# Eighteen gates slots of seven products instead of fourteen, eleven of them with weight differences made ahead and kept in DRAM

## The chip, the cores and the metric

The kernel runs on one core of one Trainium2 chip. The engines of a core work side by side, each on a queue of its own: TensorE (PE) multiplies matrices from SBUF into the eight PSUM banks, VectorE (DVE) does elementwise work, ScalarE (ACT) does copies and activations, GpSimd (POOL) does next to nothing here, and SyncE (SP) issues nearly all DMAs. The metric is the device time of one execution in microseconds (us), taken as the median of several runs.

## The reference

One decoder block on 256 tokens of width 2048, all in float32:

```python
h = rmsnorm(x, attn_norm_w)
proj = h @ w_in            # 2048 x (4*1024 + 3*1024 + 2*2048)
rq, rk, rv, rg, mq, mk, mv, g_ret, g_moba = split(proj)
o_ret  = silu(rg) * norm(retention(rotary(rq), rotary(rk), rv)) * ret_norm_w   # 4 heads of 256
o_moba = attention(rotary(mq), rotary(mk), mv)                                 # 8 heads of 128, causal
merged = sigmoid(g_ret) * (o_ret @ w_ret_up) + sigmoid(g_moba) * (o_moba @ w_moba_up)
x = x + merged @ w_out
up = causal_dwconv(rmsnorm(x, ffn_norm_w) @ w_ffn_up, conv_w, conv_b)           # 2 * 5632 columns
x = x + (silu(a) * b) @ w_ffn_down                                             # a, b = halves of up
out = rmsnorm(x, final_norm_w)
```

Nearly all of the work is the products with the weights, and each weight is used once.

## The kernel before

**Numbers in two parts.** A float32 operand is split into a high part of PE's faster format and the rest (`split2`: ACT copies the high part, DVE subtracts it and gives the low one). A product is then three matmuls: high by high, low by high, high by low.

**Slots.** The weights come as a stream of *halves*, tiles of 128 x 1024 (512 KB). Two halves are one *slot*, and the whole kernel is 252 slots in an order written out by hand. For a slot `part` splits each half of `raw` into `whi` and `wlo` and issues the load of the half four further on (`load`); there are four buffers of each kind, so the split of slot n+1 runs beside the matmuls of slot n. In a slot come, in the order of issue: the splits for the next slot, sums that are due, one stage of each running task (`run_tasks`), stages of preparation, and then the slot's matmuls, with the small matmuls of the tasks in the middle of them.

**The order of the stages.**

| slots | work |
|---|---|
| 0 to 55 | the heads: 14 groups of 4 slots, in the order mqk0, mv0, mqk2, mqk4, mv1, mqk6, rv0, rg0, rqk0, rqk1, rqk2, rqk3, rv1, rg1 |
| 56 to 103 | four chunks of 12: 8 slots of the two gates (`gr`, `gm`), 4 of the up projections (`um`, `ur`) |
| 104 to 119 | `w_out` |
| 120 to 207 | `w_ffn_up`, 22 groups of 4 slots |
| 208 to 251 | `w_ffn_down` |

A group of heads accumulates in PSUM over its four slots. There are two buffers of two banks each for this (`first_pair`); a q/k group (mqk, rqk) has 512 columns twice and takes both, `acc` and `more`. In a q/k slot the matmuls of `acc` come first and those of `more` second. When a group's last slot is issued, `closed` issues what reads the banks: for a q/k group `summed`, once for `acc` and once for `more` (ACT copies one half of the columns, L421, and DVE adds the other half to it, L422); for mv and rv copies by ACT; for rg the activation Silu by ACT (L694). The attention of the heads then runs as tasks over the next slots. The first norm also is a task: it loads the rows of x (`xt`), squares them on ACT (L376), takes the power on POOL (L289), and spreads the result with the small matmuls `across` in slot 8.

**Slots of seven.** In the gates, in `w_out` and in the down part two products over 256 rows by two column blocks are one 2 x 2 block product, and some slots make it with seven products instead of eight: 21 matmuls of 512 columns instead of 24. Such a slot needs sums of the activations (`seven_sums`, kept in tiles `s`) and, of the slot's four weight blocks, four differences. `seven_parts` makes these *in place*: four subtractions on DVE of 128 x 512 (L756 to L759) in the slot ahead, then the splits of the two halves and of three more blocks (`th`, `tl`). `SEVEN_GATES` names the slots of each chunk, `SEVEN_OUT` those of `w_out`.

**Made ready.** In the down part most slots of seven have their differences from DRAM. `make_ready` fetches a slot's weights into a tile `b`, makes the four differences with three subtractions (L187, L189, L191), and stores them in `differences`; this runs in the slots of `w_ffn_up`, one subtraction a slot. When the slot's turn comes, the three extra blocks are loaded into `got` and split, and the fourth difference is loaded in the place of a quarter of `raw`.

Of the kernel before, what the change touches and what calls it, by code (L numbers as in the profile page):

```python
# [90 lines left out]

SEVEN_GATES, SEVEN_OUT = ((4, 6), (0, 2, 4, 6), (0, 2, 4, 6), (0, 2, 4, 6)), ((3, 5), (2, 4))

# [40 lines left out]
def block(ctx: ExitStack, tc: tile.TileContext, a):  # L134
# [11 lines left out]
    left, right = ExitStack(), ExitStack()  # L146
    dr = ctx.enter_context(tc.tile_pool(name="dr", bufs=1, space=bass.MemoryType.DRAM))
    ctx.enter_context(tc.manual_schedule())

    def pool(stack, name, side="left"):  # L150
        return stack.enter_context(tc.tile_pool(name=name, bufs=1, side=side))

    def f32(ap):
# [16 lines left out]
    down_at = n_halves // 2 - NFB  # L170
    ready = [i for i, (seven, _) in enumerate(down()) if seven and i not in IN_PLACE]
    ready = {2 * (down_at + i): j for j, i in enumerate(ready)}
    differences = dr.tile([len(ready), P, 4 * CW], F32, name="differences")
# [4 lines left out]

    def make_ready(j):

        n = next(n for n, i in ready.items() if i == j)
        b = wq.tile([P, 4, CW], F32, name="b", tag=f"q{j % 2}", bufs=1)
        for h in range(2):
            nc.sync.dma_start(flat(b[:, 2 * h:2 * h + 2, :]), wts[order[n + h]])
        for _ in range(3):
            yield
        nc.vector.tensor_sub(b[:, 1:4:2, :], twice(b[:, 3, :]), b[:, 1:3, :])  # L187
        yield
        nc.vector.tensor_sub(b[:, 2, :], b[:, 2, :], b[:, 1, :])  # L189
        yield  # L190
        nc.vector.tensor_sub(b[:, 0, :], b[:, 0, :], b[:, 2, :])  # L191
        yield
        yield
        nc.sync.dma_start(differences[j], flat(b))

# [4 lines left out]
    def load(n, *some):  # L200
        if n < n_halves:
            if n not in raws:
                raws[n] = rp.tile([P, 2 * CW], F32, name="raw", bufs=RAW_BUFS)
            if n - 1 in ready:
                nc.sync.dma_start(raws[n][:, :CW], wts[order[n], :, :CW])
                nc.sync.dma_start(raws[n][:, CW:], differences[ready[n - 1], :, 3 * CW:])
                return
            for w in some or spans(n):
                nc.sync.dma_start(raws[n][:, w], wts[order[n], :, w])

    def part(n, *some):
# [263 lines left out]
    def retention(fulls, h):  # L475
# [62 lines left out]
        for k, full, w in ks:  # L538
            nc.vector.scalar_tensor_tensor(ot["rl"][:, k, :], full, w, f32(ot["rh"][:, k, :]),
                                           op0=OP.mult, op1=OP.subtract)  # L540

    def flips(full, two, c, gates):

        for b in range(2):
            for i in range(2):
                w = slice((2 * b + i) * P, (2 * b + i + 1) * P)
                for t in range(NT):
                    flip(two[b][:, i * S + t * P:i * S + (t + 1) * P], full[:, t, w])
        yield
        for b in range(2):  # L550
            k = 4 * c + 2 * b
            if gates:
                if len(big["mh"]) == c:
                    big["mh"].append(big["pm"].tile([P, 4, S], F32R, name="mgh3", tag="room", bufs=1))
                split2(*(big["m" + x][c][:, 2 * b:2 * b + 2, :] for x in "hl"), pair(two[b]))
# [110 lines left out]

    def gated():

        return [big["pg"].tile([P, NT, CW], F32, name="s" + x, bufs=1 + (x == "r")) for x in "rm"]

    def middle_pool():
        assert not tasks, len(tasks)
        left.close()
        pm = big["pm"] = pool(left, "pm")
        for x in "hl":
            big["m" + x] = [pm.tile([P, 4, S], F32R, name=f"mg{x}{c}") for c in range(4 - (x == "h"))]
        big["room"] = two_of(pm.tile([P, 2, CW], F32, name="room"))
        big["tt"] = pm.tile([P, 3, CW], F32, name="tt")
        big["junk"] = pm.tile([P, CW], F32, name="junk")
        big["th"], big["tl"] = (pm.tile([P, 3, CW], F32R, name="t" + x) for x in "hl")  # L680

    def closed(kind, n, acc, more):
# [17 lines left out]
        elif kind == "up":  # L700
            if n == 0:
                assert not tasks, len(tasks)
                left.close()
                pf = big["pf"] = pool(left, "pf")
                big["gh"], big["gl"] = (pf.tile([P, NFB - 16, S], F32R, name="g" + x) for x in "hl")
# [44 lines left out]
    def seven_parts(n, tt, th, tl):  # L750
# [10 lines left out]
        split2(*parts[n + 1], q)  # L761
        if isinstance(th, list):
            for one in zip(th, tl, tt):
                split2(*one)
        else:
            split2(th, tl, tt[3])
        for i in range(2):
            load(n + i + RAW_BUFS)

    def three(tile):  # L770
# [154 lines left out]
    def middle_slots(slot):  # L925

        slots = middle()
        fa, fb = two_of(first_pair()), two_of(first_pair())
        sr, sm = gated()
        t124 = [two_of(p1.tile([P, 2, CW], F32R, name="t", tag="kq", bufs=4)) for _ in range(3)]  # L930
        th, tl = [list(x) for x in zip(*t124)]
        for i, (seven, two) in enumerate(slots):
            c, q = divmod(i, 12)
# [17 lines left out]
            if out and q == 3:  # L951
                right.close()
                big["x2"] = [x2_half(wq, f"q{i}") for i in range(2)]
                for k in ("ss2", "ss3"):
# [18 lines left out]
            if i == 8:  # L973
                middle_pool()
                th, tl = big["th"], big["tl"]
                t124 = list(zip(three(th), three(tl)))
            n = 2 * (slot + 1)
            if q == 0 and seven:
                times(r, sr)
            if i + 1 < len(slots) and slots[i + 1][0]:  # L980
                if i < 8:
                    tt = [p1.tile([P, CW], F32, name="tt", tag=x, bufs=2) for x in ("tmp", "tmp", "full")]
                else:
                    tt = three(big["tt"]) + [big["tt"]]
                seven_parts(n, tt, th, tl)
            else:
                part(n)
                part(n + 1)
            if i and q == 0:
                if not seven:  # L990
# [5 lines left out]
                else:  # L996
                    sr, sm = gated()
            if not out:
                if c == 1 and q == 2:
                    seven_sums(3, big["sums"][1][:, 1], "gr")  # L1000
                if c == D // CW - 1 and q >= 10:
                    seven_sums(q - 10, sums_tile(big["pm"], f"s{q - 8}"), "wo")
                if q == 8:
# [7 lines left out]
            else:  # L1011
                if q % 8 == SEVEN_OUT[q // 8][-1] + 1:
                    gather = gathered(at, q // 8 * 2, big["pm"].tile([P, CW], F32, name="v", bufs=1))
                    next(gather)
# [9 lines left out]
            else:  # L1024
                js = (0, 0) if two[0][0] == two[1][0] else (0, 1)
                plain_products([(k, j) for (_, k), j in zip(two, js)], lambda k: two_blocks(k, kind), at, halves)
            issue()
            slot += 1
            if not out and q == 11:
                r, fa, fb, fc = fa, fb, fc, r  # L1030
        for j, bank in ((2, fc), (3, r)):
            summed_up(bank, j)
# [20 lines left out]
    def down_slots(slot):  # L1053
# [4 lines left out]
        th, tl = [big["t"][:, x:x + 3, :] for x in (0, 3)]  # L1058
        t124 = [list(zip(three(th), three(tl)))[x] for x in (1, 2, 0)]
        room = wq.tile([P, 4, CW], F32, name="got", tag="q0", bufs=1)  # L1060
# [3 lines left out]
        for i, (seven, where) in enumerate(slots):  # L1064
# [10 lines left out]
            if next_seven and n not in ready:  # L1075
                assert not seven
                full = big["got"][done % 2]
                seven_parts(n, [three(full)[x] for x in (1, 2, 0)] + [full], th, tl)
                get_differences(done + 2)
# [93 lines left out]
    sevens = [2 * (down_at + i) for i, (seven, _) in enumerate(down()) if seven]  # L1173
    slot, makers = 0, []
    for kind, n, _, _, rows in groups:
        if kind == "gr" and n == 0:
# [11 lines left out]
        for kc in range(nk // 4):  # L1188
            for h in range(2):
                part_x(4 * slot + 4 + 2 * h)  # L1190
                part(2 * slot + 2 + h)
            if kind == "rg" and n == 1 and kc > 0:
                if kc == 1:
# [5 lines left out]
            if kind == "up" and n in SUMS_IN_UP and kc in (1, 3):  # L1199
# [3 lines left out]
                else:  # L1203
                    big["room"] = two_of(big["wb"])
                    seven_sums(k, big["s4"])
            run_tasks()
            if kind == "up":
                j, at = divmod(2 * n + kc - 8, 5)
                if at == 0 and j in ready.values():
                    makers.append(make_ready(j))  # L1210
                for one in list(makers):
                    if next(one, makers) is makers:
                        makers.remove(one)
                if n == NFB - 2 and kc > 1:
                    get_sums(kc - 2, ("wb", "wa")[kc - 2])
            halves = [parts.pop(2 * slot + h) for h in range(2)]
# [80 lines left out]
```

## Time and profile before

| | us |
|---|---|
| median of 3 runs (lowest, highest) | 1412.05 (1412.01, 1412.32) |
| the profiled execution: its time | 1412.28 |
| the profiled execution: its span, first to last instruction | 1410.5 |
| TensorE busy in the span | 1399.3 |
| VectorE busy | 1130.9 |
| ScalarE busy | 782.0 |
| mean granted clock of TensorE | 0.999 |

The page of the profile tells of one execution. Its first part has each engine's busy time, its share of the span and the number of instructions (x). A row of the views by group has the line of the kernel, the engine, the operation, what is written <- what is read, the shapes, and the count; then the busy us, the mean ns of one, and the idle us ahead of them with what ended them. A row of the timeline has the start in us from the span's start, the duration in us, engine, line and operation, and in brackets the idle time ahead and what ended it. A row of the waits has the waiter <- what it waited for, and us in total, times, and the longest. A row of the windows has the stretch, its length, each engine's busy us with its instructions, the granted clock, the DMAs' share, and GB/s. The slots start at the first matmul of each: slot 8 at 51.2, slot 36 at 220.2, slot 40 at 243.7, slot 44 at 268.3, slot 48 at 293.4, slot 56 at 340.8 us.

### The profile page before, as it was taken

The numbers are of one execution on the slowest core, as the hardware profiler recorded it, in microseconds if no ns is written. First come the engines' busy times: TensorE is split into PE (matmuls) and PEld (weight loads), VectorE is DVE, ScalarE is ACT, GpSimd is POOL, SyncE is SP. The second block draws the span as 40 slices with busy tenths as digits, with TensorE's granted clock in tenths as the row PEclk, the third lists the DMA queues.
The fourth block names the chain that finished last, engine by engine and source line by source line (L and its number), as shares of the span: only waits on it lengthen the run. The fifth ranks groups of instructions, "written<-read, shape, count | busy, mean of one in ns | idle before, by whom it ended". The sixth has DMA issues, their size and how long they took to land.

```text
span 1410.5 us, 19509 instructions
## 1 busy us (share of the span) xinstructions
PE 1399.3 (99%) x7194; PEld 1198.2 (85%) x7194; DVE 1130.9 (80%) x1526; ACT 782.0 (55%) x1027; POOL 5.6 (0%) x14
## 2 busy tenths in 40 slices
PE   9999999999999999999999999999999999999997
PEld 7888888888888888888888888888888888888886
DVE  6687656866888989788768898898888988887767
ACT  6555454545556555555556555565555656655653
POOL 0000000000000000000000000000000000000000
PEclk9999999999999999999999999999999999999999
DMA  8755555555566566576486887887787777997894
GB/s 297 265 180 168 172 182 177 171 188 166 193 200 209 190 207 193 194 239 231 161 280 218 289 283 273 292 278 270 260 289 280 257 272 264 344 334 257 292 350 142
DMA packets 92591, 335.22 MB, mean 238 GB/s; under 512 B 10416, under 2 KB 11984, under 8 KB 90448
## 3 DMA queue, kind: packets, MB, share of 16 engines
q1 hardware_dynamic: 92064, 333.19, 69.7%
q8 instruction: 56, 0.92, 0.3%
q10 hardware_dynamic: 432, 0.79, 0.2%
q14 instruction: 39, 0.32, 0.1%
HBM read 308.78 MB, written 25.17 MB: 237 GB/s over the span
## 4 chain that ended last, share of the span: by engine, by line
PE 96%; DMA 1%; DVE 1%; issue 1%; ACT 0%; SPq 0%; POOLq 0%; POOL 0%; DVEq 0%; ACTq 0%
PE acc L235 83%; PE z L235 11%; DMA raw<-in_wts 1%; PE s L235 0%; PE o L235 0%; DVE wlo L227 0%; PE rs L235 0%; PE ro L235 0%; PE z L253 0%; PE acc L253 0%; DVE x L1051 0%; PE pt L253 0%; ACT whi L226 0%; PE tr L253 0%; ACT t L226 0%
## 5 line engine op out<-in xcount | busy, mean ns | idle before, releaser
L226 ACT ACTIVATE whi<-raw 128x1024 fp32r<-128x1024 f32 (+1 forms) x505 | 523.4, 1055 | 411.2 <-PE acc L235 241.8
L227 DVE TENSOR_TENSOR wlo<-raw,whi 128x1024 fp32r<-128x1024 f32 (+1 forms) x505 | 595.5, 1218 | 178.9 <-ACT whi L226 91.5
L235 PE MATMUL acc<-xb,whi 128*128 128x512 f32 x1920 | 466.1, 392 | 1.4 <-ACT whi L226 1.4
L235 PEld LDWEIGHTS acc<-xb,whi 128*128 128x128 f32 x1920 | 350.6, 188 | 68.9 <-ACT whi L226 2.5
L235 PEld LDWEIGHTS acc<-xb,wlo 128*128 128x128 f32 x1920 | 250.9, 191 | 12.2
L235 PE MATMUL acc<-xb,wlo 128*128 128x256 f32 x1920 | 254.6, 282 | 0.0
L235 PE MATMUL acc<-whi,xb 128*128 128x512 f32 x572 | 169.3, 391 | 0.4 <-ACT gate L694 0.4
L235 PEld LDWEIGHTS acc<-whi,xb 128*128 128x128 f32 x572 | 107.3, 188 | 22.8 <-ACT gate L694 0.8
L235 PE MATMUL acc<-wlo,xb 128*128 128x512 f32 x286 | 100.8, 390 | 0.0
L235 PE MATMUL acc<-whi,gl 128*128 128x512 f32 (+1 forms) x202 | 78.2, 387 | 0.0
L235 PE MATMUL acc<-whi,gh 128*128 128x512 f32 (+1 forms) x202 | 78.2, 387 | 0.0
L235 PEld LDWEIGHTS acc<-wlo,xb 128*128 128x128 f32 x286 | 53.8, 188 | 10.6
L235 PE MATMUL acc<-wlo,gh 128*128 128x512 f32 (+1 forms) x202 | 52.5, 387 | 0.0
L227 DVE TENSOR_TENSOR t<-got,t 128x1536 fp32r<-128x1536 f32 x20 | 35.1, 1755 | 15.6 <-PE acc L235 7.9
L235 PEld LDWEIGHTS acc<-wlo,gh 128*128 128x128 f32 x202 | 37.9, 188 | 7.7
L235 PEld LDWEIGHTS acc<-whi,gh 128*128 128x128 f32 x202 | 37.9, 188 | 7.7
L235 PEld LDWEIGHTS acc<-whi,gl 128*128 128x128 f32 x202 | 37.9, 188 | 7.7
L809 ACT ACTIVATE s<-room 128x512 fp32r<-128x512 f32 x16 | 10.1, 634 | 61.2 <-DVE room L806 61.2
L235 PE MATMUL z<-whi,xb 128*128 128x512 f32 x156 | 39.6, 389 | 0.0
L226 ACT ACTIVATE t<-got 128x1536 fp32r<-128x1536 f32 x20 | 29.7, 1486 | 17.3 <-PE acc L235 16.3
L604 DVE SCALAR_TENSOR_TENSOR ub<-ub,vec 128x256 f32<-128x256 f32 x88 | 36.7, 479 | 0.0
L604 DVE SCALAR_TENSOR_TENSOR ua<-ua,vec 128x256 f32<-128x256 f32 x88 | 36.7, 478 | 0.0
(313 smaller groups left out, 1605.4 us busy)
## 6 DMA issues: line engine op xcount, KB each, us to landing
raw<-in_wts SPq DMA_DIRECT2D x488, 512.0 KB, 4.5
b<-in_wts SPq DMA_DIRECT2D x30, 512.0 KB, 7.0
differences<-b SPq DMA_DIRECT2D x15, 1024.0 KB, 8.1
got<-differences SPq DMA_DIRECT2D x15, 768.0 KB, 6.6
s<-sums_kept SPq DMA_DIRECT2D x12, 512.0 KB, 6.9
sums_kept<-s SPq DMA_DIRECT2D x10, 512.0 KB, 6.8
raw<-in_wts SPq DMA_DIRECT2D x17, 256.0 KB, 5.2
raw<-differences SPq DMA_DIRECT2D x15, 256.0 KB, 5.5
```

Of the source, the lines that this page charges most:

```text
L226: nc.scalar.activation(hi, full, AF.Copy)
L227: nc.vector.tensor_sub(lo, full, f32(hi))
L235: to.append(lambda: nc.tensor.matmul(out, a, b, **kw))
L604: nc.vector.scalar_tensor_tensor(y[:, j, :], u[:, j, i:i + S], cv[j][:, i:i + 1], y[:, j, :], op0=OP.mult, op1=OP.add)
L809: nc.scalar.activation(hi, sums, AF.Copy)
```

## The change

Chunk 0 of the gates has slots of seven at 4, 5, 6 (were 4, 6), the other three chunks at 0, 2, 4, 5, 6 (were 0, 2, 4, 6). Of these eighteen, seven are still made in place (`SUMS_AT_ONCE`, counted from the first gates slot: 4, 14, 16, 26, 28, 38, 40), and eleven get their differences from DRAM: slots 5 and 6 of every chunk, and slot 0 of the last three.

The eleven are made in the heads. `PREPARED_AT` has the slot in which each one's three subtractions are issued, now in one piece, behind that slot's tasks and ahead of its matmuls and of `closed`; the fetch (two DMAs of 512 KB) is issued three slots ahead, or two slots behind the subtractions of the last user of the buffer, and the store (1 MB) one slot later. Two new tiles on the right side of SBUF hold first `b` and then `got`. `get_gate` loads three blocks (768 KB) of a ready slot, the first two in slot 55 and each further one when its tile is free; `split_gate` splits them in the slot ahead, ahead of that slot's matmuls or, where that slot is itself one of seven, behind them. The in-place slots use the idle quarter of the `got` tiles and `room` for their temporaries, and split the three blocks one by one.

The sums of the activations for k = 0 and 1 stay in slots 53 and 54; k = 2 goes from slot 55 to the second gates slot, k = 3 from chunk 1 to slot 9 of chunk 0, and k = 4 is new, in slot 10. The sums for `w_out` and some scratch tiles lie elsewhere; the last x tile is taken anew behind the middle (`renew_x`).

```diff
-SEVEN_GATES, SEVEN_OUT = ((4, 6), (0, 2, 4, 6), (0, 2, 4, 6), (0, 2, 4, 6)), ((3, 5), (2, 4))
+SEVEN_GATES, SEVEN_OUT = ((4, 5, 6),) + ((0, 2, 4, 5, 6),) * 3, ((3, 5), (2, 4))
+GATES_AT, SUMS_AT_ONCE = 56, (4, 14, 16, 26, 28, 38, 40)
+PREPARED_AT = (6, 7, 19, 23, 27, 31, 34, 35, 39, 43, 47)
...
+        steps = [
+            fetch,
+            lambda: nc.vector.tensor_sub(b[:, 1:4:2, :], twice(b[:, 3, :]), b[:, 1:3, :]),
+            lambda: nc.vector.tensor_sub(b[:, 2, :], b[:, 2, :], b[:, 1, :]),
+            lambda: nc.vector.tensor_sub(b[:, 0, :], b[:, 0, :], b[:, 2, :]),
+            lambda: nc.sync.dma_start(differences[j], flat(b))]
+        for step, wait in zip(steps, waits + (0,)):
+            step()
+            for _ in range(wait):
+                yield
...
+    def get_gate(j):
+        if j < len(PREPARED_AT):
+            if j < 2:
+                got.append(rt.tile([P, 4, CW], F32, name="got", tag=("pa", "pb")[j], bufs=1))
+            nc.sync.dma_start(flat(got[j % 2][:, :3, :]), differences[j, :, :3 * CW])
+
+    def split_gate(n, th, tl):
+        j = ready[n]
+        full = got[j % 2][:, :3, :]
+        if isinstance(th, list):
+            for i in range(3):
+                split2(th[i], tl[i], full[:, i, :])
+        else:
+            split2(th, tl, full)
+        get_gate(j + 2)
...
-            if i + 1 < len(slots) and slots[i + 1][0]:
+            if i + 1 < len(slots) and slots[i + 1][0] and n not in ready:
...
             else:
                 part(n)
                 part(n + 1)
+                if n in ready and not seven:
+                    split_gate(n, th, tl)
...
-                if c == 1 and q == 2:
-                    seven_sums(3, big["sums"][1][:, 1], "gr")
+                if c == 0 and q in (1, 9, 10):
+                    k = (1, 9, 10).index(q) + 2
+                    seven_sums(k, gate_sums(k) if k < 4 else sums_tile(big["pm"], "g4"), "gr")
...
             issue()
+            if n in ready and seven:
+                split_gate(n, th, tl)
...
-            if kind == "rg" and n == 1 and kc > 0:
+            if kind == "rg" and n == 1 and kc in (1, 2):
...
             run_tasks()
+            if slot in fetched_at:
+                j = fetched_at[slot]
+                b = rt.tile([P, 4, CW], F32, name="b", tag=("pa", "pb")[j % 2], bufs=1)
+                makers.append(make_ready(j, b, (PREPARED_AT[j] - slot, 0, 0, 1)))
...
+            for one in list(makers):
+                if next(one, makers) is makers:
+                    makers.remove(one)
+            if slot == GATES_AT - 1:
+                get_gate(0)
+                get_gate(1)
```

More of the change, by code (lines that the diff above doesn't have):

```diff
@@ L151, in pool @@
         return stack.enter_context(tc.tile_pool(name=name, bufs=1, side=side))
+    rt = pool(above, "rt", "right")
     def f32(ap):
@@ L170, in block @@
     down_at = n_halves // 2 - NFB
-    ready = [i for i, (seven, _) in enumerate(down()) if seven and i not in IN_PLACE]
-    ready = {2 * (down_at + i): j for j, i in enumerate(ready)}
+    ready = [GATES_AT + i for i, (seven, two) in enumerate(middle())
+             if seven and two[0][0][0] == "gr" and i not in SUMS_AT_ONCE]
+    assert len(ready) == len(PREPARED_AT)
+    ready += [down_at + i for i, (seven, _) in enumerate(down()) if seven and i not in IN_PLACE]
+    ready = {2 * i: j for j, i in enumerate(ready)}
     differences = dr.tile([len(ready), P, 4 * CW], F32, name="differences")
@@ L177, in flat, with make_ready, fetch @@
         return tile.rearrange("p a b -> p (a b)")
-    def make_ready(j):
+    def make_ready(j, b, waits):
         n = next(n for n, i in ready.items() if i == j)
[L182 to L194, printed above, removed]
+        def fetch():
+            for h in range(2):
+                nc.sync.dma_start(flat(b[:, 2 * h:2 * h + 2, :]), wts[order[n + h]])
+        steps = [
[8 more added lines that the diff above has]
+                yield
     def spans(n):
@@ L540, in retention, with renew_x @@
                                            op0=OP.mult, op1=OP.subtract)
+    def renew_x():
+        x = px.tile([P, 6, 2, S], F32R, name="xb3", bufs=1)
+        for j in range(3):
+            xtiles[5 + j] = x[:, 2 * j:2 * j + 2]
+        for k in range(10, KD):
+            xb[k] = xtiles[k // 2][:, k % 2]
+            xh[k], xl[k] = xb[k][:, 0, :], xb[k][:, 1, :]
     def flips(full, two, c, gates):
@@ L703, in closed @@
                 left.close()
+                right.close()
+                above.close()
                 pf = big["pf"] = pool(left, "pf")
@@ L979, in middle_slots @@
                 times(r, sr)
-            if i + 1 < len(slots) and slots[i + 1][0]:
-                if i < 8:
-                    tt = [p1.tile([P, CW], F32, name="tt", tag=x, bufs=2) for x in ("tmp", "tmp", "full")]
+            if i + 1 < len(slots) and slots[i + 1][0] and n not in ready:
+                if out:
+                    tt = got[0][:, :3, :]
+                    tt = turned_round(three(tt)) + [tt]
                 else:
-                    tt = three(big["tt"]) + [big["tt"]]
+                    tt = [got[0][:, 3, :], got[1][:, 3, :], big["room"][0]]
                 seven_parts(n, tt, th, tl)
@@ L1077, in down_slots @@
                 full = big["got"][done % 2]
-                seven_parts(n, [three(full)[x] for x in (1, 2, 0)] + [full], th, tl)
+                seven_parts(n, turned_round(three(full)) + [full], th, tl)
                 get_differences(done + 2)
```

53 lines of the change are left out of this document (34 added, 19 removed).

## The prediction

> **What bounds the kernel.** I read the page's busy row and chain first, then the waits of TensorE (PE) alone, then short windows of single slots.
>
> ```profile
> PE 1399.3 (99%) x7194; PEld 1198.2 (85%) x7194; DVE 1130.9 (80%) x1526; ACT 782.0 (55%) x1027; POOL 5.6 (0%) x14
> PE 96%; DMA 1%; DVE 1%; issue 1%; ACT 0%; SPq 0%; POOLq 0%; POOL 0%; DVEq 0%; ACTq 0%
> ```
>
> ```profile
> PE acc L235 <- ACT whi L226: 1.4, 3, 0.7
> ...
> PE acc L235 <- ACT gate L694: 0.4, 1, 0.4
> ```
>
> PE is busy for 99% of the span, carries 96% of the chain, and its longest waits are 1.4 and 0.4 us in total. So time changes by two things only: matmuls that go, and new gaps in front of PE. VectorE (DVE) at 80% is no bound, but at places it has little room, and there it can make such a gap. The sum is made on one execution of 1412.28 us (span 1410.5), 0.23 above the median of 1412.05; I add the differences to the median.
>
> **The matmuls that go.** These windows are cut at the first matmuls of slots: a gates slot of seven, the plain slot after it, and two slots of seven in a row in the down part.
>
> ```profile
> 364.20:368.96 4.76, 4.76 (x22) 3.94 (x21) 4.50 (x7) 2.32 (x3) 0.00 (x0) 1.00 0.71 239
> 368.96:374.40 5.44, 5.44 (x25) 4.50 (x24) 4.62 (x6) 3.49 (x5) 0.00 (x0) 1.00 0.59 209
> 1212.70:1222.25 9.55, 9.55 (x44) 7.91 (x43) 8.70 (x7) 5.68 (x6) 0.00 (x0) 1.00 0.96 350
> ```
>
> A plain slot (24 matmuls) takes 5.44, one of seven (21) takes 4.76: 0.68 us less, or 3 x 0.227. Four more slots of seven: **-2.72 us**. The gates will now have three slots of seven in a row. The third row shows two in a row at 4.77 each, with no PE wait, where the second has its differences from DRAM as here: there t's low half of 1.75 us is written behind the matmuls of the first and is in time. A third one repeats this step, so I put no loss on it.
>
> **DVE in the gates.** The first row is the whole second chunk from its second slot to its eighth, the other two are the pieces of work that change.
>
> ```profile
> 411.20:447.20 36.00, 36.00 (x161) 29.80 (x160) 34.16 (x41) 20.24 (x20) 0.00 (x0) 1.00 0.61 200
> ```
>
> ```profile
> L757 DVE TENSOR_TENSOR raw<-raw 128x512 f32<-128x512 f32 x23 | 15.9, 692 | 0.8
> L227 DVE TENSOR_TENSOR tl<-tt,th 128x1536 fp32r<-128x1536 f32 x16 | 28.0, 1751 | 0.0
> ```
>
> Even with 34.16 of 36.00 us busy (the sums of one k lie in it) PE had no wait. A chunk had four slots of seven made in place (four subtractions of 0.69, or 2.8 us each); now two are, and three come ready. That takes 5.5 us off DVE and adds one split of t (1.75) and two splits cut in three (about 0.3 each): 3 us less per chunk. The sums of k = 3 leave this chunk; those of k = 2, 3, 4 go to slots 1, 9 and 10 of the first. In slot 1 there is room:
>
> ```profile
> 352.66 1.23 DVE L227 TENSOR_TENSOR wlo<-raw,whi 128x1024 fp32r<-128x1024 f32 x1 [2.38 <-issue]
> ```
>
> Slots 9 and 10 get about 2.5 us each, and slot 11 loses the 2.8 of an in-place preparation. If that cover fails, the next chunk's first slot waits; I take nothing, bounds 0 to 0.5. The subtractions' temporaries in the idle quarter of the ready tiles, the output sums in the x tile, and the pools only move storage: nothing, as each is released slots before.
>
> **A stall that goes.** At the seam from the last head group to the gates PE waits for a bank that ScalarE (ACT) reads:
>
> ```profile
> 340.59 2.20 PE L235 MATMUL acc<-whi,xb 128*128 128x512 f32 x9
> 343.16 2.14 PE L235 MATMUL acc<-whi,xb 128*128 128x512 f32 x8 [0.36 <-ACT gate L694]
> ```
>
> ```profile
> 341.32 0.63 ACT L809 ACTIVATE s<-room 128x512 fp32r<-128x512 f32 x1 [3.14 <-DVE room L806]
> 341.86 1.25 ACT L694 ACTIVATE gate<-acc,r 128x512 f32<-128x512 f32 x2
> ```
>
> Nine matmuls at 0.227 end their issue at 342.63; the next came at 343.16, and a second short hold followed (0.11). The gate's activations stood behind the sums' L809, which waited 3.14 us for DVE. These sums (k = 2) leave that slot, so the gate can start when PE is done, about 341.0, and ends at 342.3, in time: **-0.64 us** (bounds -0.64 and 0).
>
> **The eleven preparations.** Each is three subtractions in one piece in slot 6, 7, 19, 23, 27, 31, 34, 35, 39, 43 or 47:
>
> ```profile
> L187 DVE TENSOR_TENSOR b<-b 128x1024 f32<-128x1024 f32 x15 | 18.3, 1217 | 0.0
> L189 DVE TENSOR_TENSOR b<-b 128x512 f32<-128x512 f32 x15 | 10.3, 684 | 0.0
> L191 DVE TENSOR_TENSOR b<-b 128x512 f32<-128x512 f32 x15 | 10.2, 683 | 0.0
> ```
>
> 2.58 us together. They stand behind the slot's tasks and ahead of what `closed` issues at the group's end. For a q/k group, that is `summed`: ACT copies one half of acc, DVE adds the other (L422). A q/k group takes both pairs of acc banks, so the next group's first matmul writes the banks that L422 reads. The queue is in order: what is late on DVE then is late on PE. At the ends of slots 35, 39, 43, 47 (DVE, then PE's first matmul of the next slot):
>
> ```profile
> 215.50 1.22 DVE L227 TENSOR_TENSOR wlo<-raw,whi 128x1024 fp32r<-128x1024 f32 x1
> 218.20 0.69 DVE L422 TENSOR_TENSOR rfull<-acc,rfull 128x512 f32<-128x512 f32 x1 [1.49 <-ACT rfull L421]
> 220.16 0.63 PE L235 MATMUL acc<-xb,whi 128*128 128x512 f32 x2
> 240.96 0.29 DVE L503 TENSOR_TENSOR sd<-rest 128x128 f32<-128x128 f32 x1
> 241.74 0.69 DVE L422 TENSOR_TENSOR rfull<-acc,rfull 128x512 f32<-128x512 f32 x1 [0.49 <-ACT rfull L421]
> 243.71 0.40 PE L235 MATMUL acc<-xb,whi 128*128 128x512 f32 x1
> 266.55 0.68 DVE L422 TENSOR_TENSOR rfull<-acc,rfull 128x512 f32<-128x512 f32 x1
> 268.31 0.40 PE L235 MATMUL acc<-xb,whi 128*128 128x512 f32 x1
> 291.59 0.68 DVE L422 TENSOR_TENSOR rfull<-acc,rfull 128x512 f32<-128x512 f32 x1
> 293.35 0.40 PE L235 MATMUL acc<-whi,xb 128*128 128x512 f32 x1
> ```
>
> - Slot 35: DVE free at 216.72, with 2.58 at 219.30, L422 ends at 219.99; PE comes at 220.16. No gap, 0.17 to spare.
> - Slot 39: 241.25 + 2.58 + 0.69 = 244.52 against 243.71: 0.81.
> - Slot 43: no idle ahead of L422, so it ends 2.58 later, 269.81 against 268.31: 1.50.
> - Slot 47: 294.85 against 293.35: 1.50.
>
> With the hand-over seen above (gate's end 343.11, PE 343.16) 0.05 more each: **+3.96 us**. At the other slots the group's end is read by ACT alone, or there are no tasks (23 and the earlier ones): nothing.
>
> A rule to weigh. The Trainium skill, "Perfetto Trace Analysis", section Matmuls, has matmul groups rotate through different PSUM banks so that evacuating one overlaps the matmuls of the next. By it the evacuation would cost nothing here and the whole sum, with the last term below, would come to 1409.3 instead of 1413.2. By the rows above two pairs rotate inside one group, so the next group meets the banks just filled; the trace does not agree at these seams.
>
> **DMAs and SP.** Each preparation adds two fetches, a store and a load of three quarters, and one split load, all issued by SP.
>
> ```profile
> b<-in_wts SPq DMA_DIRECT2D x30, 512.0 KB, 7.0
> differences<-b SPq DMA_DIRECT2D x15, 1024.0 KB, 8.1
> got<-differences SPq DMA_DIRECT2D x15, 768.0 KB, 6.6
> ```
>
> A fetch has 2 or 3 slots of 5.4 us or more to land: in time, also where (slot 33) it queues behind the store of the slot before and holds SP for some us. The loads of `raw` behind it have 2 slots of lead. The first two fetches are the doubt: they fall into the start.
>
> ```profile
> 27.00:34.00 7.00, 7.00 (x36) 5.92 (x35) 4.14 (x5) 4.03 (x5) 0.00 (x0) 1.00 0.69 236
> 34.00:40.00 6.00, 6.00 (x28) 4.96 (x27) 3.02 (x3) 3.16 (x4) 0.00 (x0) 1.00 0.82 262
> 40.00:52.00 12.00, 12.00 (x55) 9.93 (x54) 4.17 (x6) 7.01 (x12) 0.00 (x0) 1.00 1.00 373
> ```
>
> ```profile
> 50.45 1.06 ACT L376 ACTIVATE xt<-xt 128x1024 f32<-128x1024 f32 x1 [2.14 <-DMA xt<-in_x]
> 52.14 0.70 POOL L289 TENSOR_TENSOR r<-r1ms,mhalf 128x2 f32<-128x2 f32 x1 [51.28 <-DVE r1ms L287]
> 54.01 0.60 PE L235 MATMUL across<-ident,r 128*128 128x128 f32 x4
> ```
>
> Two fetches are 2.10 MB, 5.6 us at the 373 GB/s of the full stretch. Ahead of 40 us 31% of 7 and 18% of 6 us are free: 3.25. Up to 2.4 us of delay reach the last x row that the first norm needs; that norm is done at 52.84, PE wants it at 54.01: 1.17 of cover. So 0 to 1.2 us; I take the middle, **+0.6**, as nothing shows which packets pass first.
>
> **Sum:** -2.72 - 0.64 + 3.96 + 0.6 = +1.2; 1412.05 + 1.2 = **1413.2 us**. With the ends of the bounds this case runs from 1412.3 to 1414.8.
>
> **Rivals.**
> 1. *The seams hide the subtractions* (they run in idle time of DVE, as the low load of these slots suggests: L422 had 0.49 idle ahead in slot 39). Then -2.72 - 0.64 are left: 1408.7, and 1409.3 with the 0.6 at the start. Against it: in slots 43 and 47 no idle time precedes L422, and L422 is issued behind the subtractions. This is what the page's rule on rotating banks comes to.
> 2. *Slower: the first norm is late.* If none of the gaps ahead of 40 us can be used, the fetches hold the last x row back by 5.6, PE waits 5.6 - 1.17 = 4.4 in slot 8, and the time is 1412.05 - 3.36 + 3.96 + 4.4 = 1417.1. It decides the sign beyond 0.2% from a wait of 2.2 us. For it: full DMA from 40 to 52. Against: 0.69 and 0.82 before.
> 3. *Slots of seven that aren't 4.76 long*: in the run of three DVE must split 4.2 us per slot (two halves of 1.2, t 1.75). At half a us each for the eight slots behind another one the result is near 1417. Against it the two-in-a-row of the down part.
>
> **Chances.** My forecast 0.62, rival 1 0.20, rival 2 0.12, rival 3 0.06. 0.2% is 2.8 us, about what a measurement of this kernel can tell from no change: below 1409.2 is faster (rival 1 without the wait at the start, 0.17), above 1414.9 slower (rivals 2 and 3, 0.18), the rest same (the forecast and the other part of rival 1, 0.65). The range reaches down to rival 1 and up to the forecast's edge: 1408.6 to 1415.0.
>
> **What would show it.** Gates slots 5 and 6 at 4.76 (plain before); no PE wait on gate L694 near 342; PE gaps of about 0.9, 1.55, 1.55 at the starts of slots 40, 44, 48, put down to DVE L422, with the three subtractions right ahead of it; PE's `across` in slot 8 later than its place by up to 1.2. I am wrong if L422 ends ahead of those slots, if PE's gaps are put down to other rows, or if `across` waits beyond 2 us.

## The result and the profile after

| | before | after |
|---|---|---|
| median of 6 runs each, same chip (lowest, highest), us | 1412.07 (1411.71, 1412.43) | 1419.28 (1418.78, 1422.78) |
| the profiled execution: its time | 1412.28 | 1418.78 |
| its span | 1410.5 | 1416.6 |

The ratio is 1.0056 (95% interval 1.0045 to 1.0066): the changed kernel is slower by 7.2 us at the median, where I had forecast +1.2 and a range that ended at +3. Its runs also lie further apart (4.0 us, before 0.7); the profiled execution is the fastest of the six.

The page of the changed kernel, its busy row and chain by engine (lines are numbered anew: the matmul helper L235 is L265, the bank reads L421/L422 are L451/L452, the subtractions L187/L189/L191 are L197 to L199):

```profile
PE 1398.8 (99%) x7182; PEld 1196.4 (84%) x7182; DVE 1151.2 (81%) x1555; ACT 787.5 (56%) x1046; POOL 6.5 (0%) x14
PE 92%; DVE 3%; DMA 2%; issue 1%; ACT 1%; POOL 0%; SPq 0%; DVEq 0%; POOLq 0%; ACTq 0%
```

The busy rows hardly differ. The chain does: PE carries 92% of it where it carried 96%, and DVE 3% where it carried 1%. Which gaps these are is told by the waits of PE (in us in total, times, longest):

```profile
PE acc L265 <- DVE rfull L452: 3.7, 3, 1.4
PE acc L265 <- DVE sr L964: 1.9, 1, 1.9
PE across L265 <- POOL r L319: 1.7, 1, 1.7
PE idle L765 <- DVE idle L762: 1.2, 1, 1.2
PE acc L265 <- ACT whi L256: 1.1, 3, 0.7
```

Before, 1.4 on whi was the largest sum. The first three rows are new and the row on gate L694 is gone. Measured from the first matmul of a slot to the first of the next, every slot whose length differs by more than 0.08 us between the two profiles, the very first one left out:

| slots | what changed there | us |
|---|---|---|
| 39, 43, 47 (and a short second hold in 40, 44, 48) | L452 late | +1.07, +1.57, +1.57 (+0.35) |
| 35, 36 | L452 late | +0.22 |
| 8 | `across` late | +1.93 |
| 68, first slot of chunk 1 | `sr` L964 late | +2.16 |
| 56 | gate stall gone | -0.70 |
| 61, 73, 85, 97 | now slots of seven | -0.68 each |
| 213, 245, in the down part | neither made nor read differently | +0.09, +0.54 |

They add up to +6.1, the difference of the two spans.

**The matmuls that went.** The window of slot 61, gates slot 5 of chunk 0, reads as a slot of seven did before, and in slot 56 seventeen matmuls run in one row where nine and eight were held apart:

```profile
374.90:379.66 4.76, 4.76 (x22) 3.94 (x22) 4.17 (x5) 3.58 (x6) 0.00 (x0) 1.00 0.47 181
```

```profile
347.27 4.02 PE L265 MATMUL acc<-whi,xb 128*128 128x512 f32 x17
```

**The seam at the end of slot 39**, DVE's timeline and PE's first matmul of slot 40:

```profile
243.56 1.22 DVE L197 TENSOR_TENSOR b<-b 128x1024 f32<-128x1024 f32 x1
244.81 0.69 DVE L198 TENSOR_TENSOR b<-b 128x512 f32<-128x512 f32 x1
245.54 0.69 DVE L199 TENSOR_TENSOR b<-b 128x512 f32<-128x512 f32 x1
246.15 1.28 DVE L452 TENSOR_TENSOR rfull<-acc,rfull 128x512 f32<-128x512 f32 x2
246.89 1.42 PE L265 MATMUL acc<-xb,whi 128*128 128x512 f32 x5 [0.91 <-DVE rfull L452]
```

The three subtractions stand right ahead of L452, without a gap. Both L452 now run in one row, where the second had come more than a microsecond behind the first, and PE starts 0.05 us behind the end of the first (246.15 + 0.69 = 246.84).

**The first norm**, in the timelines of four engines:

```profile
52.51 1.06 ACT L406 ACTIVATE xt<-xt 128x1024 f32<-128x1024 f32 x1 [2.72 <-DMA xt<-in_x]
53.97 1.22 DVE L197 TENSOR_TENSOR b<-b 128x1024 f32<-128x1024 f32 x1
54.21 1.54 POOL L319 TENSOR_TENSOR r<-r1ms,mhalf 128x2 f32<-128x2 f32 x1 [53.34 <-DVE r1ms L317]
55.81 0.71 PE L265 MATMUL across<-ident,r 128*128 128x128 f32 x4 [1.68 <-POOL r L319]
```

The last row of x is squared at 52.51 where it was at 50.45: 2.06 us later. And POOL's power takes 1.54 us where it took 0.70. Beside it runs the first subtraction of slot 7's preparation: in DVE's queue it stands right behind the two small rows of the norm, which wait for that row of x, so it starts 0.24 us ahead of POOL. (Slot 6's had run at 42.75, undisturbed.) 2.06 + 0.84, less the cover of 1.17, is 1.73; PE's wait reads 1.68.

**The start of chunk 1.** DVE's timeline of after, then PE's, then the DVE rows of before that answer to the last two of DVE:

```profile
408.26 0.69 DVE L856 TENSOR_TENSOR s<-room,s 128x512 fp32r<-128x512 f32 x1 [0.70 <-ACT s L855]
408.87 1.28 DVE L964 TENSOR_TENSOR sm<-z,sm 128x512 f32<-128x512 f32 x2
410.07 2.35 DVE L257 TENSOR_TENSOR wlo<-raw,whi 128x1024 fp32r<-128x1024 f32 x2
412.33 1.75 DVE L257 TENSOR_TENSOR tl<-got,th 128x1536 fp32r<-128x1536 f32 x1
414.00 1.28 DVE L964 TENSOR_TENSOR sr<-acc,sr 128x512 f32<-128x512 f32 x2
```

```profile
412.57 1.07 PE L265 MATMUL z<-whi,s 128*128 128x512 f32 x4
415.54 0.70 PE L265 MATMUL acc<-th,s 128*128 128x512 f32 x2 [1.91 <-DVE sr L964]
```

```profile
403.24 1.75 DVE L227 TENSOR_TENSOR tl<-tt,th 128x1536 fp32r<-128x1536 f32 x1
406.57 1.29 DVE L918 TENSOR_TENSOR sr<-acc,sr 128x512 f32<-128x512 f32 x2 [1.58 <-PE acc L235]
```

The multiplication `sr` (L964, before L918) reads the banks that chunk 0 filled, and the first slot of chunk 1, one of seven, needs those banks from its ninth matmul on, 1.8 us in (slot 68 begins at 411.66, so at 413.5). Before, DVE had idled 1.58 us for PE ahead of it: it was as early as it could be. After, DVE came to it at 414.00, from a chain of work with the sums of k = 4 of slot 10 in it (405.82 to 408.95), in which it idled only for the 0.70 us inside those sums. A `tl` split stood ahead of `sr` before, too.

### The profile page after: what moved, and what is told of

It is laid out like the page before. It is cut to its first block, busy times and chain, and to the rows that moved or that the text cites. A ratio compares the mean times of both kernels' runs of the same rounds, so it can differ in the third digit from the quotient of the medians.

```text
span 1416.6 us, 19616 instructions
## 1 busy us (share of the span) xinstructions
PE 1398.8 (99%) x7182; PEld 1196.4 (84%) x7182; DVE 1151.2 (81%) x1555; ACT 787.5 (56%) x1046; POOL 6.5 (0%) x14
## 4 chain that ended last, share of the span: by engine, by line
PE 92%; DVE 3%; DMA 2%; issue 1%; ACT 1%; POOL 0%; SPq 0%; DVEq 0%; POOLq 0%; ACTq 0%
PE acc L265 79%; PE z L265 11%; DMA raw<-in_wts 2%; DVE wlo L257 1%; DMA xt<-in_x 1%; ACT whi L256 0%; PE s L265 0%; PE o L265 0%; PE ro L265 0%; DVE b L197 0%; PE acc L283 0%; PE z L283 0%; DVE x L1110 0%; PE rs L265 0%; PE pt L283 0%
## 5 line engine op out<-in xcount | busy, mean ns | idle before, releaser
L265 PE MATMUL acc<-xb,whi 128*128 128x512 f32 x1920 | 466.4, 392 | 3.3 <-DVE rfull L452 2.3
L265 PEld LDWEIGHTS acc<-xb,whi 128*128 128x128 f32 x1920 | 350.5, 188 | 71.4 <-DVE rfull L452 2.9
L265 PEld LDWEIGHTS acc<-xb,wlo 128*128 128x128 f32 x1920 | 250.9, 191 | 12.3
L265 PE MATMUL acc<-xb,wlo 128*128 128x256 f32 x1920 | 254.6, 282 | 0.0
L265 PE MATMUL acc<-whi,xb 128*128 128x512 f32 x548 | 163.8, 391 | 1.4 <-DVE rfull L452 1.4
L265 PEld LDWEIGHTS acc<-whi,xb 128*128 128x128 f32 x548 | 102.8, 188 | 22.7 <-DVE rfull L452 1.6
L265 PE MATMUL acc<-wlo,xb 128*128 128x512 f32 x274 | 98.2, 390 | 0.0
L265 PE MATMUL acc<-whi,gl 128*128 128x512 f32 (+1 forms) x202 | 78.2, 387 | 0.0
L265 PE MATMUL acc<-whi,gh 128*128 128x512 f32 (+1 forms) x202 | 78.2, 387 | 0.0
L265 PEld LDWEIGHTS acc<-wlo,xb 128*128 128x128 f32 x274 | 51.5, 188 | 10.2
L257 DVE TENSOR_TENSOR t<-got,t 128x1536 fp32r<-128x1536 f32 (+1 forms) x28 | 40.2, 1450 | 18.1 <-PE acc L265 13.2
L265 PE MATMUL acc<-wlo,gh 128*128 128x512 f32 (+1 forms) x202 | 52.5, 387 | 0.0
L256 ACT ACTIVATE t<-got 128x1536 fp32r<-128x1536 f32 (+1 forms) x28 | 34.2, 1239 | 21.6 <-PE acc L265 20.6
L265 PEld LDWEIGHTS acc<-wlo,gh 128*128 128x128 f32 x202 | 37.9, 188 | 7.7
L265 PEld LDWEIGHTS acc<-whi,gh 128*128 128x128 f32 x202 | 37.9, 188 | 7.7
L265 PEld LDWEIGHTS acc<-whi,gl 128*128 128x128 f32 x202 | 37.9, 188 | 7.7
L257 DVE TENSOR_TENSOR tl<-got,th 128x1536 fp32r<-128x1536 f32 (+1 forms) x25 | 30.5, 1241 | 8.1 <-PE z L265 5.5
```

Of the source, the lines that this page charges most:

```text
L256: nc.scalar.activation(hi, full, AF.Copy)
L257: nc.vector.tensor_sub(lo, full, f32(hi))
L265: to.append(lambda: nc.tensor.matmul(out, a, b, **kw))
```

## The experiments

Three theories were open. *Queue*: each new wait is what DVE's order of issue makes of it, so that it goes when the rows ahead of the late one are moved. *Load*: the work added to DVE and the transfers added to the DMAs are the cost, wherever they stand. *Split*, for slot 68 alone: not the sums but the `tl` split of the ready slot, directly ahead of L964, is what makes it late. Each edit is against the changed kernel unless it says otherwise.

### The last three preparations one slot earlier

```diff
-PREPARED_AT = (6, 7, 19, 23, 27, 31, 34, 35, 39, 43, 47)
+PREPARED_AT = (6, 7, 19, 23, 27, 31, 34, 35, 38, 42, 46)
```

> The last three preparations are made one slot earlier (38, 42, 46 instead of 39, 43, 47); all else is the changed kernel. Queue theory (PE waits at a few places, each because of what stands ahead in one engine's queue): L422 at the ends of slots 39, 43, 47 is no longer behind the subtractions, the three waits on it (3.7 us, 4.2 to 4.7 with the hand-over around them) go, and the time falls from 1419.3 to about 1414.8. Load theory (the added work of VectorE, 1151 against 1131 us, and of the DMAs, 74.5 against 69.7 per cent, costs what the matmuls save, wherever it stands): the same work in other slots, so the time stays within 1 us of 1419.3.

Measured: 1414.15 (1411.91 to 1416.11, 10 runs) against 1412.02, ratio 1.0012 (1.0003 to 1.0021). Its profiled execution took 1412.14, one of the faster. All its waits on PE:

```profile
PE acc L265 <- DVE sr L964: 2.1, 1, 2.1
PE idle L765 <- DVE idle L762: 1.2, 1, 1.2
PE across L265 <- POOL r L319: 0.8, 1, 0.8
PE acc L265 <- ACT whi L256: 0.3, 1, 0.3
```

The row on L452 is gone, and slots 35 to 48 all have their old lengths. DVE in slot 38 and at the end of slot 39:

```profile
237.62 1.23 DVE L197 TENSOR_TENSOR b<-b 128x1024 f32<-128x1024 f32 x1 [2.50 <-issue]
...
243.48 0.68 DVE L452 TENSOR_TENSOR rfull<-acc,rfull 128x512 f32<-128x512 f32 x1
```

The same subtractions on the same bytes one slot earlier lie in 2.50 us of idle time and cost nothing. *Queue* holds for these three seams; *load* as a whole does not. Slot 35 is back at its old length although its preparation did not move, so its 0.22 us have another cause: in the changed kernel its fetch landed at 218.76 and DVE idled 0.24 us until 218.84 for it; here it landed at 217.47 and DVE did not idle. The other two waits stay, so they are separate.

### The same three slots, but behind the bank reads

The stages of preparation of slots 39, 43 and 47 are issued behind `closed` instead of ahead of the matmuls:

```diff
-            for one in list(makers):
+            held = slot in (39, 43, 47)
+            for one in list(makers) if not held else []:
...
         closed(kind, n, acc, more)
+        for one in list(makers) if held else []:
+            if next(one, makers) is makers:
+                makers.remove(one)
```

> The preparations stay in slots 39, 43, 47, but their three subtractions are issued behind what the group's end issues, instead of ahead of it. Queue theory: the order alone decides; L422 ends ahead of the next slot as in the kernel before, the three waits go, and the time is about 1415; the splits that come behind may lose up to 2.6 us of lead, which they have. Load theory: VectorE has the same work in the same slots, so the time stays within 1 us of 1419.3.

Measured: 1415.59 (1413.84 to 1418.32, 10 runs), ratio 1.0023 (1.0014 to 1.0033). Slots 39 and 47 have no wait. Two of its waits on PE, and ACT's first split for slot 44:

```profile
PE acc L265 <- DVE rfull L452: 0.6, 1, 0.6
PE acc L265 <- DVE wlo L257: 0.5, 1, 0.5
```

```profile
266.56 1.06 ACT L256 ACTIVATE whi<-raw 128x1024 fp32r<-128x1024 f32 x1 [4.99 <-DMA raw<-in_wts]
```

The place in the queue alone takes most of it away; the count of instructions, the slots and the number of DMAs are those of the changed kernel. Two pieces come back. Slot 50 is 1.27 longer, since the subtractions behind slot 47 now stand ahead of the next slots' splits and the rows of the next tasks. Slot 43 is 0.80 longer than before the change with no subtraction ahead of its L452, and this one is the DMAs': the task rows ahead of L452 stand behind the split of slot 44's weights, which waits for their load. That load landed 7.01 us after its issue where it took 3.68 in the kernel before; ahead of it in SP's queue stand the store of slot 39's differences, issued 3.6 us later than in the changed kernel because the subtractions are, and two fetches. So here a part of *load* is true. The Trainium skill, "PSUM — Partial Sum Buffer", section "Engine vs sequencer instructions", calls the queues of ScalarE and VectorE strictly first in, first out; this pair of runs agrees with it: the subtractions issued ahead of L452 delayed it, those issued behind did not.

### The first two subtractions later, behind the first norm

```diff
-PREPARED_AT = (6, 7, 19, 23, 27, 31, 34, 35, 39, 43, 47)
+PREPARED_AT = (8, 12, 19, 23, 27, 31, 34, 35, 39, 43, 47)
...
-        fetched_at[max(at - 3, PREPARED_AT[j - 2] + 2 if j > 1 else 0)] = j
+        fetched_at[max(at - 3, PREPARED_AT[j - 2] + 2) if j > 1 else (3, 4)[j]] = j
```

The fetches stay in slots 3 and 4.

> The first two fetches stay in slots 3 and 4; their subtractions (and stores) go from slots 6 and 7 to 8 and 12. Queue theory: of the wait of the matmuls 'across' for the first norm (1.7 us), the part from the DMAs stays (the last row of x lands 2.06 us late) and the part from POOL goes (its power took 1.54 us beside the subtraction of VectorE, 0.70 before): the wait falls to about 0.9 and the time by about 0.8 to 1418.5; slot 15 may lose up to 0.3. If the DMAs alone make the wait, it stays at 1.7; if the subtractions alone make it, it goes and the time is 1417.4.

Measured: 1420.32 (1418.41 to 1421.02, 4 runs), ratio 1.0052 (1.0037 to 1.0067): no faster than the changed kernel. POOL and PE at the first norm, and one of the waits on PE:

```profile
54.84 0.70 POOL L319 TENSOR_TENSOR r<-r1ms,mhalf 128x2 f32<-128x2 f32 x1 [53.98 <-DVE r1ms L317]
55.60 0.71 PE L265 MATMUL across<-ident,r 128*128 128x128 f32 x4 [1.08 <-POOL r L319]
```

```profile
PE acc L265 <- DVE mfull L452: 1.6, 1, 1.6
```

Without a subtraction beside it, POOL's power is back at 0.70. The last row of x still comes late (its squares start at 53.15), so `across` still waits: the two parts of that wait are separate, and the larger is the fetches'. My expected time was missed by 1.8 us, for two reasons that the profile shows. The subtractions moved into slot 8 push the rows of the next head's tasks until L452 at the end of slot 11 comes late (slot 11 +1.80). And in this execution the wait at slot 39 was 2.45 where it had been 1.07 (the reason is told below).

### No preparation at the start at all

```diff
-PREPARED_AT = (6, 7, 19, 23, 27, 31, 34, 35, 39, 43, 47)
+PREPARED_AT = (19, 22, 23, 27, 30, 31, 34, 35, 39, 43, 47)
```

> The changed kernel with preparations in 19, 22, 23, 27, 30, 31, 34, 35, 39, 43, 47: nothing is fetched in the start any more; the waits at slots 40, 44, 48 and 68 are left in. Queue theory: the wait for across goes with its spread (1.7 us in the first profile, 0.8 to 2.8 in five), so about 1417.2, with runs within 1 us of each other. If the spread of the changed kernel has another cause (the DMAs of the down part), it stays at 3 to 4 us.

Measured: 1416.57 (1416.40 to 1418.61, 4 runs), ratio 1.0035 (1.0022 to 1.0049). POOL at the first norm and DVE from slot 34 to the end of slot 35:

```profile
51.31 0.70 POOL L319 TENSOR_TENSOR r<-r1ms,mhalf 128x2 f32<-128x2 f32 x1 [50.44 <-DVE r1ms L317]
...
212.36 1.23 DVE L197 TENSOR_TENSOR b<-b 128x1024 f32<-128x1024 f32 x1 [1.10 <-DMA b<-in_wts]
...
217.75 1.23 DVE L197 TENSOR_TENSOR b<-b 128x1024 f32<-128x1024 f32 x1 [0.21 <-DMA b<-in_wts]
...
220.35 1.28 DVE L452 TENSOR_TENSOR rfull<-acc,rfull 128x512 f32<-128x512 f32 x2
```

Slot 8 has its old length: all of that wait came from the two preparations at the start. The seam at slot 35 is what took its place: slot 34's fetch, issued in slot 32 where it was slot 31, lands at 212.23 where it landed at 203.61, DVE waits 1.10 us for the one of slot 34 and 0.21 for the one of slot 35, and slot 35 is 1.13 longer. Slots 43 and 47 cost 1.57 each, as in the changed kernel. The median is 0.6 below what I expected. The spread of 1 us did not come true: three runs lie within 0.3 us and one is 2.2 above the lowest. That one has a lower mean clock (0.997, the others 0.998 and 0.999), of which more below.

### The sums of k = 4 elsewhere

```diff
-                if c == 0 and q in (1, 9, 10):
-                    k = (1, 9, 10).index(q) + 2
+                if (c, q) in ((0, 1), (0, 9), (1, 2)):
+                    k = (1, 9, 2).index(q) + 2
```

> The sums of k = 4 are made in slot 2 of chunk 1 instead of slot 10 of chunk 0. Queue theory: the products with sigmoid at the start of chunk 1 (sr, L964) are no longer late, PE's wait of 1.9 us at the first slot of chunk 1 goes, and the time falls by about 2.1 to 1417.2. If that wait is rather from the split of the ready blocks (1.75 us directly ahead of it on VectorE), it stays, and the time is 1419.3.

Measured: 1416.12 (1415.61 to 1419.22, 7 runs), ratio 1.0031 (1.0019 to 1.0042). DVE at the start of chunk 1 (the profiled execution is the slowest of the seven, with 4.4 us more in slot 8 than before the change):

```profile
413.18 1.75 DVE L257 TENSOR_TENSOR tl<-got,th 128x1536 fp32r<-128x1536 f32 x1
415.31 1.29 DVE L964 TENSOR_TENSOR sr<-acc,sr 128x512 f32<-128x512 f32 x2 [0.38 <-PE acc L265]
```

The `tl` split is still there, and L964 now waits for PE, 0.38 us. Slot 68 is back at its old 4.79. So it was the sums in slot 10, and *split* falls. The room is small, though: 0.38 us of idle time is left where there were 1.58.

### The gate stall by itself, in the kernel before

Only the sums of k = 2 go from slot 55 to the second gates slot of the kernel before:

```diff
+                if c == 0 and q == 1:
+                    seven_sums(2, gate_sums(2), "gr")
...
-            if kind == "rg" and n == 1 and kc > 0:
+            if kind == "rg" and n == 1 and kc in (1, 2):
```

> The kernel before with one part of the change alone: the sums of k = 2 are made in the second gates slot instead of slot 55. Queue theory: the gate's activations no longer stand behind the sums on ACT, PE's 0.64 us at slot 56 go: 1411.4. If the stall has another cause: 1412.0.

Measured: 1411.46 (1410.89 to 1412.03, 11 runs) against 1412.18, ratio 0.9996 (0.9987 to 1.0005). The time alone can't be told from no change. The slot can: PE runs through where it was held twice.

```profile
340.37 4.01 PE L235 MATMUL acc<-whi,xb 128*128 128x512 f32 x17
```

Slot 56 is 0.70 shorter, as in every kernel that has this move.

### All of it, with every preparation in a slot that has room

```diff
-PREPARED_AT = (6, 7, 19, 23, 27, 31, 34, 35, 39, 43, 47)
+PREPARED_AT = (19, 22, 23, 27, 30, 31, 34, 38, 42, 46, 51)
```

and the sums of k = 4 in slot 2 of chunk 1, as above.

> The changed kernel with its eleven preparations in slots 19, 22, 23, 27, 30, 31, 34, 38, 42, 46, 51 (no early fetch, none in the last slot of a q/k group that has tasks) and the sums of k = 4 in slot 2 of chunk 1. Queue theory: the three kinds of wait are gone (across, L422, sr L964), the four slots of 4.76 and the gate's stall remain as gains: 1412.0 - 2.72 - 0.7 = 1408.6, with runs as close together as those of the kernel before. Load theory: all of the added work is still there, so the time is not below 1412.

Measured: 1408.95 (1408.20 to 1409.72, 11 runs) against 1412.18 (26 runs), ratio 0.9977 (0.9968 to 0.9985). Its busy row and all its waits on PE:

```profile
PE 1397.4 (99%) x7182; PEld 1196.8 (85%) x7182; DVE 1151.1 (82%) x1555; ACT 787.6 (56%) x1046; POOL 7.4 (1%) x14
```

```profile
PE idle L765 <- DVE idle L762: 1.2, 1, 1.2
PE acc L265 <- ACT whi L256: 0.5, 1, 0.5
PE acc L265 <- ACT t L256: 0.2, 1, 0.2
```

DVE does the same 1151 us of work as in the changed kernel, PE carries 96% of the chain again, and the one wait on DVE that is left, on the tile named idle, read 1.2 us in the kernel before as well. Against the kernel before, besides slot 0, only slots 56, 61, 73, 85 and 97 (-0.70 and four times -0.68) and slot 245 (+0.10) differ by more than 0.08. This version is 3.2 us faster than the kernel before on the same chip; the changed kernel was 7.2 slower than it on its own.

### One preparation at the start

As the last, but slot 22's preparation goes to slot 6 and its fetch to slot 3:

```diff
-PREPARED_AT = (19, 22, 23, 27, 30, 31, 34, 38, 42, 46, 51)
+PREPARED_AT = (6, 19, 23, 27, 30, 31, 34, 38, 42, 46, 51)
```

> As e4_all, but the preparation of slot 22 is made in slot 6 instead, with its fetch of 1 MB in slot 3. If the DMAs have the free time ahead of 40 us that the shares of the kernel before show (0.31 of 7 us and 0.18 of 6), one fetch of 2.8 us is taken in and the last row of x lands no more than 0.6 us later, within the 1.17 us of cover: the time of e4_all within 0.3. If a fetch in that stretch delays the row by its whole length, the wait for across is up to 1.7 us and the time is 1409 to 1410.5, with more spread.

Measured: 1408.88 (1408.12 to 1409.48, 10 runs), ratio 0.9977 (0.9968 to 0.9986): the same as without it. POOL and PE at the first norm, and the DMAs in the first two windows of the prediction (share of the DMAs and GB/s stand last):

```profile
52.34 0.70 POOL L319 TENSOR_TENSOR r<-r1ms,mhalf 128x2 f32<-128x2 f32 x1 [51.47 <-DVE r1ms L317]
53.32 0.60 PE L265 MATMUL across<-ident,r 128*128 128x128 f32 x4
```

```profile
27.00:34.00 7.00, 7.00 (x36) 5.93 (x35) 4.64 (x5) 3.56 (x4) 0.00 (x0) 1.00 0.96 348
34.00:40.00 6.00, 6.00 (x28) 4.97 (x27) 2.50 (x3) 3.28 (x5) 0.00 (x0) 1.00 0.96 312
```

The free 31% and 18% of these stretches are now filled, and the last row of x is squared at 50.65, 0.2 us later than before, counted from the span's start. One fetch of 1.05 MB, 2.8 us at 373 GB/s, fits in the 3.25 us that were free. In the changed kernel the second fetch was issued at 35.37 and landed at 44.26, in the full stretch. Nor is there much left with one: slot 8 begins 0.69 us earlier in this execution, so against PE the row is 0.9 later, and POOL ends at 53.04, 0.28 ahead of `across`, where the cover was 1.17.

## Why the prediction was wrong

**The sum missed by 4.9 us** between the profiled executions (+6.1 against +1.2), and three terms missed in the same direction: 2.16 for DVE in the gates, 1.33 for the start and 0.82 for the preparations. Of the signs that I had named for being wrong one came: a gap of PE put down to another row, `sr` L964. The gate stall gave 0.06 more than forecast, and 0.63 stand in two slots of the down part that I had no term for.

- *The matmuls that go, -2.72*: right. Slots 61, 73, 85, 97 went from 5.44 to 4.76; the third slot of seven in a row cost nothing, which drops rival 3. What I wrote on where to look named gates slots 5 and 6 as plain before; slot 6 had been one of seven already, only slot 5 was new.
- *The gate stall, -0.64*: right, -0.70, and it stays -0.70 when that move is made alone.
- *The eleven preparations, +3.96*: right in mechanism and place, a little small. By slots 39, 43, 47: 0.86, 1.55, 1.55 told with the hand-over, 1.07, 1.57, 1.57 measured. A second short hold of 0.11 to 0.14 in the next slot, which I had not counted, adds 0.35, and slot 35, where I had 0.17 to spare, lost 0.22 with slot 36. Together 4.78. The waits are there, so rival 1, the seams that hide everything, fell; and moving the subtractions one slot earlier removed them.
- *DMAs and SP, +0.6 with bounds 0 to 1.2*: the bound failed. The fetches' part came near its upper end: 2.06 us of delay where I had allowed 2.4. What broke the bound was a second cost in the same place: slot 7's subtractions stand right behind the norm's last DVE row, start 0.24 us ahead of POOL's power, and that went from 0.70 to 1.54. I had priced these subtractions on DVE alone, and the trace of before has no such pair of rows. Slot 8 lost 1.93. This is a weak form of rival 2 (4.4 us), below the 2.2 that I gave as its point of decision. Not in every execution: with the sums of k = 4 moved, the start untouched, the profile's wait for `across` is 2.77.
- *DVE in the gates, nothing, bounds 0 to 0.5*: **this is the step that failed most**, by 2.16 us in slot 68. I had written that slots 9 and 10 get 2.5 us each and slot 11 loses 2.8, that is, I compared sums of work over three slots with their length. The question that decides is another: what must DVE have finished at a given moment? The first slot of a chunk needs the banks that `sr` reads 1.8 us after it begins, and before the change `sr` started as soon as PE let it. Any backlog at that moment is PE's wait. The row that shows it, DVE's `sr` with 1.58 us of idle time ahead, stood in the trace of before: 1.58 of idle and 0.3 behind it (it ends at 407.86; slot 68 began at 406.37 and eight matmuls of 0.227 end at 408.19) is all the room there was. The sums of k = 4 hold DVE for 3.1 us, from 405.82 to 408.95 in the trace of after: the 2.5 that I had counted, and 0.70 of waiting for ACT in the middle.

**Late transfers at slots 35 and 39.** Two of the sizes above go back to the sentence that the fetches and the loads behind them are in time. Slot 35's fetch was not, by 0.24 us (see the run on the last three preparations). And at slot 39 the store and the fetches that SP issues in slot 36 stand ahead of the loads of slot 40's weights. In the changed kernel the first of these loads landed 7.4 us after its issue, before 3.5; ACT's split waited for it:

```profile
239.05 1.06 ACT L256 ACTIVATE whi<-raw 128x1024 fp32r<-128x1024 f32 x1 [5.21 <-DMA raw<-in_wts]
```

DVE's half of that split, the task rows and the subtractions all come behind it. In the four profiles with these subtractions in slot 39 the load landed 8.1, 6.9, 6.3 and 5.5 us ahead of the moment at which PE would have begun slot 40 without a wait, and slot 39 was longer by 0.78, 1.07, 1.67 and 2.45: the later the load, the longer the slot. At slots 43 and 47 of the changed kernel the split doesn't wait for its load, and the slots are longer by what I had forecast, within 0.02.

Two slips in the working change nothing in this. The ends of the bounds add up to 1412.65 and 1415.0, not 1412.3 and 1414.8. And the second longest wait of before is not 0.4 us but 1.2, on the tile idle; it is the same after.

Of the 7.2 us at the medians, 6.1 stand between the spans, 0.4 lie outside them (6.5 between the times of the profiled executions), and 0.7 is that these executions stand 0.2 above and 0.5 below their medians.

**The spread.** The kernels with both preparations at the start and their subtractions in slots 6 and 7 (the changed one and the runs on the seams, the order and the sums) spread over 3.6 to 4.5 us, the two final versions over 1.5 and 1.4. In the four profiled executions of the first kind slot 8 is longer by 1.93, 1.04, 3.63 and 4.40 us, the last row of x being squared at 52.51, 51.44, 52.54 and 54.22. The first and the third differ by 1.70 us with the row at the same place. The granted clock tells them apart (it stands behind POOL's busy time); the first row is of the changed kernel, the second of the run on the order:

```profile
57.00:60.00 3.00, 3.00 (x18) 2.63 (x18) 3.00 (x3) 2.01 (x2) 0.00 (x0) 1.00 0.52 147
57.00:60.00 3.00, 3.00 (x11) 2.43 (x10) 1.94 (x2) 1.47 (x2) 0.00 (x0) 0.50 0.38 85
```

In the run on the order and in that on the sums, right behind the wait for `across` (1.81 and 2.77 us), the clock is 0.50 for 3.41 us, which is 1.71 us of PE's time. The other two profiles read 1.00 there. So the long waits of the start cost more than themselves in some executions. The mean clock of every run fits: 3.41 us at half lower it by 0.0012, and of the 27 runs on the seams, the order and the sums, 11 read 0.997, at medians 2.7 to 3.0 us above the other runs of the same kernel. None of 80 runs of the kernel before, of the gate alone and of the two final versions reads below 0.998. Of the changed kernel's six runs four read 0.997 or 0.996, and the profiled one is not among them.

**Open.** What decides whether the clock falls: it did behind waits of 1.81 and 2.77 us and did not behind one of 2.30 (slot 39, in the run with the first two subtractions later). Slots 213, 221 and 245 of the down part differ by up to 0.54 us from before, 245 with both signs, in the kernel with the gate alone too; I have no cause for it.

## What to carry to other kernels

When an engine that isn't the bound gets more work, its free time per stage is the wrong measure: list the few moments at which the bound engine needs something from it (banks to be read at a seam, a scale for a norm), and check that none of the new work stands in the queue ahead of that, nor a new transfer ahead of the loads it needs. Three preparations moved by one slot each were worth 4.6 us here, more than the 3.4 that the change gains. And after removing a wait, look who was second: three of the five single moves here made a new wait elsewhere.

## What the runs showed of the hardware

POOL's power on 128 x 2 took 0.70 us in the kernel before and wherever it ran alone, and 1.54 to 1.55 in the four profiles where DVE's subtraction of 128 x 1024 ran beside it. A second case, in the kernel with the last three preparations earlier:

```profile
52.90 1.23 DVE L197 TENSOR_TENSOR b<-b 128x1024 f32<-128x1024 f32 x1
53.13 1.55 POOL L319 TENSOR_TENSOR r<-r1ms,mhalf 128x2 f32<-128x2 f32 x1 [52.27 <-DVE r1ms L317]
```

In both, POOL ends about 0.55 us behind the end of the subtraction (54.13 and 54.68 here, 55.19 and 55.75 in the changed kernel), as though it had waited for it, while DVE's own rows kept their 1.22 and 0.69. The Trainium skill, "SBUF — State Buffer", section "Who interferes with whom", says that a DVE instruction with two SBUF inputs contends with a GpSimd instruction that reads SBUF, and that issue order decides who blocks; these two cases, in which DVE started 0.24 and 0.23 us earlier, agree, as far as ends and starts can show it.

The granted clock of PE fell to 0.50 for 3.41 us in two profiles, behind PE waits of 1.81 and 2.77 us, and stayed at 1.00 behind one of 2.30.

Weight loads that stood in SP's queue behind a store of 1 MB and two fetches of 512 KB landed 7.0 to 8.5 us after their issue (the first load for slot 40 in four profiles, for slot 44 in the run on the order); in the kernel before, with neither ahead of them, they took 3.5 and 3.7.
